# Layer 1, last block: the gate as an item of the weights' stream, second weights ahead of the half sums, the context tile third

## The chip, the cores and the metric

The kernel runs on one core of a Trainium2 chip. The time is microseconds of device time for one launch; before the change it is 1283.76 us (median of 3 runs, 1283.36 to 1283.88).

## The reference, cut to what matters

Two layers; the second one (layer 1) ends with a squared-ReLU MLP, an adaLN gate, a residual add and the final RMSNorm:

```python
def squared_relu_mlp(h, w1, w2):
    a = jax.nn.relu(h @ w1)
    return (a * a) @ w2
...
        x = x + g1 * mix
        h = rms_norm(x, norm2_g[l]) * (1 + sc2) + sh2
        x = x + g2 * squared_relu_mlp(h, w_ff1[l], w_ff2[l])
    return rms_norm(x, final_g), ckv_list, kpe_list
```

512 latent tokens and 128 context tokens, D = 1024, D_FF = 4096. Latent and context tokens have different gates g2.

## The kernel before, in words

Tokens stand in five tiles of 128: 0 to 3 are latent, 4 is context. Every product in float32 is made of three matmuls: each operand is split into a high part (rounded to fp32r) and a low part (the rest), and `mm3` (L823 to L825) adds high·high, high·low and low·high in one PSUM bank. There are six such banks for this part of the program.

A weight comes through the class `Weights`, a stream of items in a fixed order. `loads` issues the load of a raw tile on SP's queue as soon as one of five raw buffers is free (L185); `pump` takes the next item, lets ACT write the high part (L213) and lets DVE subtract it for the low part (L223). With no engine for the low part, ACT writes the negated high part (L216) and a DMA from GpSimd's queue adds the raw weight from HBM to it (L220). DVE's subtraction is put in a list, `lag`, and issued by `lows` at the next `pump`, so that ACT's copy is done by then. The first weights of layer 1's later blocks are items `w1s`: quarter combinations of one block, seven for each half block p (ACT L576, DVE L581 and, for the sources, L583).

The MLP has eight blocks of 512 hidden columns. In layer 1 the up-projection of a block's half (`up7`) is seven products of twelve matmuls of 320 columns in place of eight, with DVE adds between them (L1632); ACT makes relu, square and the high part, DVE the low part (L1637 to L1644). The down-projection (`down_t`) takes a token tile t and a half q of the 1024 output columns: four k, twelve matmuls of 512 columns. Before each block's down-projection four "half sums" (k = 0 and 1 only, six matmuls each) are made for the first four pairs (t, q), while the second half block's activations are still being made.

All engines run their instructions in the order in which this code emits them; a transfer queue keeps its order as well. In the last block (b = 7) the order is written out by hand: the gate row of the latent tokens (`gate_load(0)`, L2020) is loaded into a raw buffer before the second half block; `more` puts eight multiplications y·gate (L2032), two after each of four steps, and for each a GpSimd DMA that adds the residual x from HBM to y (L2033), between the steps of that half block. After the half sums come the context gate and the final gain (L2020, L2024), and then the pairs in the order of LASTS = (4, 3, 2, 0, 1). For tile 4 y gets the product's sum first and the gate after it (L1738, L2032); for the others the sum is multiplied by the gate and added to y (`last_more`: L2042, L2043). `last_sq` squares on ACT (L2057) and multiplies by the gain on DVE (L2059); `last_out` makes the reciprocal root and scales and stores. The first `last_out` is for three tiles together.

Of the kernel before, what the change touches and what calls it, by code (L numbers as in the profile page):

```python
# [44 lines left out]
POOL_AT = 6  # L45
H512 = slice(0, 512)
TAIL = slice(0, 256), slice(256, 512)
PARKS = 0, 1, 4, 3, 2
PARK_AT = {(0, 4): 1, (0, 5): 1, (0, 6): 1, (0, 7): 1, (1, 4): 1, (1, 5): 2, (1, 6): 2, (1, 7): 1}
MID = {6: (2, 1, 0, 3)}  # L50
# [81 lines left out]
class Weights:  # L132
# [3 lines left out]
    def __init__(self, nc, raw):  # L136
        self.nc, self.raw = nc, raw
        self.items, self.loaded, self.done = [], 0, 0
        self.raw_live, self.raw_cap, self.tiles, self.of = 0, RAWB, {}, {}
        self.raws = {}  # L140
        self.slots = None
        self.caps = {}

        self.lo = nc.vector
        self.own = {}
        self.hold = None
        self.slow = ()
        self.later, self.skip = [], False
        self.keep, self.second = {}, None
        self.lag, self.lagging = [], False  # L150
# [40 lines left out]
    def pump(self, n=1):  # L191

        if self.skip:
            self.skip = False
            return
        while n > 0 and self.done < len(self.items):
            self.lows()
            key, loads, size, use = self.items[self.done]
            own = self.own.get(key)
            if (use is None or key[0] == "w1s") and own is None and self.full(key) or key == self.hold:  # L200
                return
            self.loads()
            if self.done not in self.raws:
                return
            ts = self.raws.pop(self.done)
            if use is None:
                if own is None:
                    self.of[key], w = self.slots.take([128, 2, 1024], F32R)
                else:
                    w = own()  # L210
                r = ts[0][:, 0:size]
                hi, lo = w[:, 0, 0:size], w[:, 1, 0:size]
                self.nc.scalar.activation(out=hi, in_=r, func=AF.Copy)  # L213
                eng = None if key[0] in self.slow else self.lo
                if eng is None:
                    self.nc.scalar.activation(out=lo, in_=hi.bitcast(F32), func=AF.Copy, scale=-1.0)  # L216
                    src, shape = loads[0]
                    if len(shape) == 2:
                        lo = lo.rearrange("p (k n) -> p k n", k=shape[0])
                    self.nc.gpsimd.dma_start(out=lo, in_=src, accum_op=ALU.add)  # L220
                else:
                    self.lag.append(
                        lambda: eng.tensor_tensor(out=lo, in0=r, in1=hi.bitcast(F32), op=ALU.subtract)  # L223
                    )
                self.tiles[key] = w
                rest = None
            else:
                rest = use(ts)
            self.done += 1
            for f in self.later:  # L230
                f[0] -= 1
            self.flush(0)
            if rest:

                self.skip = False
                d = self.done
                self.pump()
                rest()
                self.skip = self.done > d
            n_raw = self.keep.pop(key, len(loads))  # L240
            self.lag.append(lambda: self.used(n_raw))
            if not self.lagging:
                self.lows()
            n -= 1
# [42 lines left out]
def body(ctx, tc, a):  # L287
# [316 lines left out]
    def add_w2(l, b):  # L604
        for k in range(FB):
            r = (b * FB + k) * 128
            st.add(("w2", l, b, k), [(a["w_ff2"][l, r:r + 128, :], (1024,))], 1024)

    add_w1(0, 0)
    vm = vmods(1)  # L610
    for b in range(1, NFB + 1):
# [13 lines left out]
    for b in range(NFB):  # L625
        if b >= 2:
            add_w1s(1, b)
        add_w2h(1, b)


# [838 lines left out]
    def mlp(l, C, H, lead, CL, per_d, per_c, mid, tick=None, turn=None, seven=False):  # L1469
# [124 lines left out]

        def up7(b, p, last=False):
            n = C[0][1]
            gates = [(t, q) for t in LASTS[1:] for q in range(2)] if last else []

            def more(k=1):
                for t, q in gates[0:k]:  # L1600
# [49 lines left out]
            p1 = new("p1")  # L1650
            act(out=p1, in_=pa, func=AF.Copy)
            pd = product(1, 2, None, True)
            st.pump()
            pb = product(2, 1, None, True)
            u2, u3 = new("u2"), new("u3")
            add(u2, p1, pb)
# [27 lines left out]
        def blocks7(f0):  # L1684

            st.lagging = True
            for b in range(NFB):
                if b >= f0:
                    for p in range(FB // 2):
                        if b == NFB - 1 and p:  # L1690
                            gate_load(0, rawp.tile([128, 1024], F32, tag="raw", name="G"))
                        up7(b, p, b == NFB - 1 and p == 1)

                cut = (lambda todo: {i: down_t(b, *i, H512, None, False, (0, 1)) for i in todo})
                if b < f0:
                    for k in (2 * b, 2 * b + 1):
                        bg.add(sums(k, room(k)))
                if b < NFB - 1:
                    todo = [(t, q) for q in range(2) for t in LASTS]
                    early = cut(todo[0:4]) if b >= f0 else {}  # L1700
                    for j, (t, q) in enumerate(todo):
                        ps = early.pop((t, q), None)
                        ps = down_t(b, t, q, H512, ps, True, range(FB) if ps is None else (3, 2))
                        y = tile_q(t, q)
                        if b == 3 and j == 0:
                            gate_rows()
                        if b == 0:
                            act(out=y, in_=cols(ps), func=AF.Copy)
                        else:
                            vec.tensor_tensor(out=y, in0=cols(ps), in1=y, op=ALU.add)  # L1710
                        bg.step(2)
                        if j == 4:
                            free2(b, 0)
                        if j:
                            st.pump(1 + j % 2)
                    free2(b, 1)
                    if b == f0 - 1:
                        bg.drain()
                    continue

                todo = [(t, q) for t in LASTS for q in range(2)]
                st.pump(4)
                early = cut(todo[0:4])
                w = st.slots.take([128, 2, 1024], F32)[1]
                gate_load(1, w[:, 0])
                gain_load(w[:, 1])
                zs = [fa.tile([128, 2, T], F32, tag="aa", name="z").rearrange("p a n -> p (a n)") for _ in range(3)]
                st.slots.free += cell["spare"]
                zs += [st.slots.take([128, 2, 1024], F32)[1].rearrange("p a n -> p (a n)") for _ in range(2)]
                cell["zs"] = [z[:, 0:1024] for z in zs]  # L1730
                for t, q in todo:
                    i = LASTS.index(t)
                    for v in TAIL if (t, q) == todo[-1] else (H512,):
                        ps = early.pop((t, q), None)
                        ps = down_t(b, t, q, v, ps, True, range(FB) if ps is None else (3, 2))
                        if not i:
                            y = tile_q(t, q)
                            vec.tensor_tensor(out=y, in0=cols(ps), in1=y, op=ALU.add)  # L1738
                            last_gate(t, (q,))
                        else:  # L1740
                            last_more(t, q, v, ps)
                            last_sq(t, q, v, q + (v.start > 0))
                    if q and i == 2:

                        for k in range(2):
                            last_sq(LASTS[0], k, H512, k)
                        last_out(LASTS[0:3], False)
                    elif q and i > 2:
                        last_out(LASTS[i:i + 1], i == 4)

        spare = []

# [266 lines left out]
    def gate_load(m, out):  # L2019
        nc.sync.dma_start(out=out, in_=grow[m:m + 1, :].to_broadcast([128, D]))  # L2020
        cell["G", m] = out
# [23 lines left out]
    def last_sq(t, q, v, i):  # L2045
# [1 line left out]
        k = slice(v.start // 128, v.stop // 128)  # L2047
        y = tile_q(t, q)[:, k]
        if (t, "ss") not in cell:
            i3 = LASTS.index(t)  # L2050
            if ("ss", i3 // 3) not in cell:
                cell["ss", i3 // 3] = sc.tile([128, 8], F32, tag="m", name=f"ss{t}", bufs=10)
            cell[t, "ss"] = cell["ss", i3 // 3][:, i3 % 3 * 2:]
            cell[t, "z"] = cell["zs"].pop(0)
# [4 lines left out]
        vec.tensor_tensor(out=cols(cell[t, "z"][:, u]), in0=y, in1=cols(cell["fg"][:, u]), op=ALU.mult)  # L2059

    def last_out(ts, both):
        i3, n = LASTS.index(ts[0]), len(ts)
        ss = cell["ss", i3 // 3]
        i3 %= 3
        sm = sc.tile([128, 8], F32, tag="m", name=f"sm{ts[0]}", bufs=10)[:, 0:n]
# [14 lines left out]
                eng.dma_start(out=a["y"][tok(t), u], in_=y)  # L2080

    xT = dr.tile([T, D], F32, name="xT")
    grow = dr.tile([2, D], F32, name="grow")
    LASTS = (4, 3, 2, 0, 1)

    def pool_mm(ci, N, gs=POOL_ORDER):
# [184 lines left out]
```

## Time and profile before

| | |
|---|---|
| median of 3 runs | 1283.76 us |
| the profiled execution itself | 1285.38 us |
| its span, first to last instruction | 1283.6 us |
| TensorE (PE) busy | 1247.0 us, 97% |
| VectorE (DVE) busy | 796.9 us, 62% |
| ScalarE (ACT) busy | 571.1 us, 44% |
| GpSimd (POOL) busy | 198.5 us, 15% |
| TensorE's mean granted clock | 0.988 of full speed |

The span is what the profile's views count from; 1.8 us of the profiled execution lie outside it, and the execution is 1.6 us above the median. PE's share is an average: the stretch to look at is the last block, from about 1219 us to the end. There a row of a timeline reads: start, duration, engine, line of the kernel, operation, tiles out<-in, shape, and in brackets the idle time before it and what ended that. A matmul's duration overlaps that of the next one, so the distance between two starts is what one costs.

### The profile page before, as it was taken

The numbers are of one execution on the slowest core, as the hardware profiler recorded it, in microseconds if no ns is written. First come the engines' busy times: TensorE is split into PE (matmuls) and PEld (weight loads), VectorE is DVE, ScalarE is ACT, GpSimd is POOL, SyncE is SP. The second block draws the span as 40 slices with busy tenths as digits, with TensorE's granted clock in tenths as the row PEclk, the third lists the DMA queues.
The fourth block names the chain that finished last, engine by engine and source line by source line (L and its number), as shares of the span: only waits on it lengthen the run. The fifth ranks groups of instructions, "written<-read, shape, count | busy, mean of one in ns | idle before, by whom it ended". The sixth has DMA issues, their size and how long they took to land. (4 is left out here: it accounts for less than half of the span.)

```text
span 1283.6 us, 19571 instructions
## 1 busy us (share of the span) xinstructions
PE 1247.0 (97%) x7744; PEld 1135.7 (88%) x7744; DVE 796.9 (62%) x1455; ACT 571.1 (44%) x1022; POOL 198.5 (15%) x181
## 2 busy tenths in 40 slices
PE   6999999999999999999999999899999999999986
PEld 4899975689999999999999999889898989989875
DVE  5753854554766566666666637775576556675667
ACT  4445654543554434334332424745444515445154
POOL 0010122212122221313131314210000000000030
PEclk9999999999999999999999999899999999999988
DMA  7752696250344443535353441904113343132273
GB/s 297 262 167 68 152 254 235 97 197 1 120 139 139 124 154 119 158 121 159 120 161 118 142 139 29 234 27 128 60 33 100 83 82 96 37 122 76 66 128 102
DMA packets 79163, 161.89 MB, mean 126 GB/s; under 512 B 7728, under 2 KB 34864, under 8 KB 78560
## 3 DMA queue, kind: packets, MB, share of 16 engines
q1 hardware_dynamic: 69296, 145.94, 35.6%
q0 software_dynamic: 9344, 14.35, 6.2%
q8 instruction: 61, 1.00, 0.3%
q10 hardware_dynamic: 432, 0.35, 0.1%
q14 instruction: 30, 0.25, 0.1%
HBM read 149.46 MB, written 8.02 MB: 123 GB/s over the span
## 5 line engine op out<-in xcount | busy, mean ns | idle before, releaser
L823 PE MATMUL up_ps<-h,w 128*128 128x320 f32 (+2 forms) x800 | 251.8, 315 | 4.7 <-DVE r L1632 3.1
L824 PE MATMUL up_ps<-h,w 128*128 128x320 f32 (+2 forms) x800 | 249.4, 312 | 1.2 <-DVE h L774 1.2
L825 PE MATMUL up_ps<-h,w 128*128 128x320 f32 (+2 forms) x800 | 249.9, 312 | 0.0
L213 ACT ACTIVATE w<-raw 128x1024 fp32r<-128x1024 f32 (+4 forms) x131 | 132.8, 1027 | 109.6 <-DMA raw<-w_ff 84.1
L223 DVE TENSOR_TENSOR w<-raw,w 128x1024 fp32r<-128x1024 f32 (+4 forms) x122 | 151.5, 1249 | 48.0 <-ACT w L213 47.1
L823 PEld LDWEIGHTS up_ps<-h,w 128*128 128x128 f32 x800 | 152.4, 190 | 9.1 <-issue 6.7
L823 PE MATMUL dn_ps<-aa,w 128*128 128x328 f32 (+1 forms) x512 | 159.1, 311 | 0.0
L824 PE MATMUL dn_ps<-aa,w 128*128 128x328 f32 (+1 forms) x512 | 159.0, 311 | 0.0
L825 PE MATMUL dn_ps<-aa,w 128*128 128x328 f32 (+1 forms) x512 | 158.1, 309 | 0.0
L824 PEld LDWEIGHTS up_ps<-h,w 128*128 128x128 f32 x800 | 152.7, 191 | 1.9 <-DVE h L774 1.6
L825 PEld LDWEIGHTS up_ps<-h,w 128*128 128x128 f32 x800 | 152.2, 190 | 0.3 <-DMA w<-w_ff 0.3
L484 POOL TENSOR_TENSOR acc<-acc,raw 128x1024 f32<-128x1024 f32 x42 | 100.7, 2397 | 303.7 <-ACT raw L482 303.7
L824 PE MATMUL dn_ps<-w,aa 128*128 128x512 f32 (+1 forms) x324 | 126.1, 389 | 2.4 <-DVE w L223 2.4
L823 PE MATMUL dn_ps<-w,aa 128*128 128x512 f32 (+1 forms) x324 | 126.8, 391 | 0.0
L825 PE MATMUL dn_ps<-w,aa 128*128 128x512 f32 (+1 forms) x324 | 126.3, 390 | 0.0
L1429 DVE SCALAR_TENSOR_TENSOR x<-dn_ps,mod,x 128x328 f32<-128x328 f32 (+2 forms) x168 | 67.3, 435 | 68.0 <-PE dn_ps L825 67.3
L576 ACT ACTIVATE w<-raw 128x512 fp32r<-128x512 f32 x84 | 51.0, 625 | 120.5 <-DVE raw L583 120.5
L823 PEld LDWEIGHTS dn_ps<-aa,w 128*128 128x128 f32 x512 | 96.4, 188 | 1.8 <-ACT r L1502 0.8
L825 PEld LDWEIGHTS dn_ps<-aa,w 128*128 128x128 f32 x512 | 96.3, 188 | 0.0
L824 PEld LDWEIGHTS dn_ps<-aa,w 128*128 128x128 f32 x512 | 96.2, 188 | 0.1
L482 ACT ACTIVATE raw<-raw,cs 128x1024 f32<-128x1024 f32 x42 | 48.3, 1150 | 62.5 <-DVE acc L477 58.0
L824 PEld LDWEIGHTS dn_ps<-w,aa 128*128 128x128 f32 x324 | 61.3, 189 | 15.5 <-DVE w L223 2.8
(403 smaller groups left out, 2421.1 us busy)
## 6 DMA issues: line engine op xcount, KB each, us to landing
raw<-w_ff SPq DMA_DIRECT2D x126, 512.0 KB, 3.8
raw<-w_mod SPq DMA_DIRECT2D x80, 512.0 KB, 3.9
raw<-w_m SPq DMA_DIRECT2D x16, 512.0 KB, 6.5
raw<-w_out SPq DMA_DIRECT2D x8, 512.0 KB, 4.5
w<-w_ff POOLq DMA_DIRECT2D x8, 512.0 KB, 9.8
kT<-ckvT POOLq DMA_DIRECT2D x4, 768.0 KB, 11.0
xr<-x SPq DMA_DIRECT2D x5, 512.0 KB, 6.2
xs<-x SPq DMA_DIRECT2D x2, 1280.0 KB, 10.1
```

The source lines that it names most:

```text
L213: self.nc.scalar.activation(out=hi, in_=r, func=AF.Copy)
L223: lambda: eng.tensor_tensor(out=lo, in0=r, in1=hi.bitcast(F32), op=ALU.subtract)
L482: act(out=raw if k else acc[1], in_=raw, func=AF.Copy, scale=w[1])
L484: nc.gpsimd.tensor_tensor(out=acc[1], in0=acc[1], in1=raw, op=ALU.add)
L576: act(out=w[:, 0], in_=src, func=AF.Copy)
L823: mm(ps, lhsT=st_[0], rhs=mv[0], start=first, stop=False, skip_group_check=on)
L824: mm(ps, lhsT=st_[0], rhs=mv[1], start=False, stop=False, skip_group_check=on)
L825: mm(ps, lhsT=st_[1], rhs=mv[0], start=False, stop=last, skip_group_check=on)
L1429: vec.scalar_tensor_tensor(out=xv, in0=ps[:, p0:p0 + c1 - c0], scalar=gate[:, d, m:m + 1], in1=xv, op0=ALU.mult, op1=ALU.add)
```

## The change

The latent tokens' gate is an item `("gate",)` of the stream, ahead of the last block's second weights; it has no work of its own, and its raw buffer is kept to the end (`keep` 0). The first two second weights of that block (k = 0 and 1, both halves q) get their low part by ACT and a GpSimd DMA (`st.dma`) in place of DVE. One pump in the last half block takes two items, so all four second weights are pumped before the half sums, and `lows` issues the last subtraction there too. The order is ENDS = (3, 2, 4, 0, 1); the gate multiplications of tiles 3, 2 and 0 stay in the half block, those of tiles 4 and 1 come behind the half sums; tile 4 goes the way of the others (`last_more`, `last_sq`).

```diff
+ENDS = 3, 2, 4, 0, 1
...
-                eng = None if key[0] in self.slow else self.lo
+                eng = None if key[0] in self.slow or key in self.dma else self.lo
...
+        if b == NFB - 1:
+
+            st.add(("gate",), [(grow[0:1, :].to_broadcast([128, D]), (D,))], 0, lambda ts: cell.update({("G", 0): ts[0]}))
+            st.keep["gate",] = 0
+            st.dma = [("w2", 1, b, 0, h) for h in range(2)]
         add_w2h(1, b)
...
-            gates = [(t, q) for t in LASTS[1:] for q in range(2)] if last else []
+            gates = [(t, q) for t in ENDS[0:2] + ENDS[3:4] for q in range(2)] if last else []
...
             pd = product(1, 2, None, True)
-            st.pump()
+            st.pump(1 + last)
             pb = product(2, 1, None, True)
...
-                        if b == NFB - 1 and p:
-                            gate_load(0, rawp.tile([128, 1024], F32, tag="raw", name="G"))
...
-                todo = [(t, q) for t in LASTS for q in range(2)]
-                st.pump(4)
+                todo = [(t, q) for t in ENDS for q in range(2)]
+                st.pump(5)
+                st.lows()
                 early = cut(todo[0:4])
...
+                last_gate(NT - 1)
+                last_gate(ENDS[-1])
                 for t, q in todo:
-                    i = LASTS.index(t)
+                    i = ENDS.index(t)
...
-                        if not i:
-                            y = tile_q(t, q)
-                            vec.tensor_tensor(out=y, in0=cols(ps), in1=y, op=ALU.add)
-                            last_gate(t, (q,))
-                        else:
-                            last_more(t, q, v, ps)
-                            last_sq(t, q, v, q + (v.start > 0))
-                    if q and i == 2:
-
-                        for k in range(2):
-                            last_sq(LASTS[0], k, H512, k)
-                        last_out(LASTS[0:3], False)
-                    elif q and i > 2:
-                        last_out(LASTS[i:i + 1], i == 4)
+                        last_more(t, q, v, ps)
+                        last_sq(t, q, v, q + (v.start > 0))
+                    if q and i >= 2:
+                        last_out(ENDS[0:3] if i == 2 else ENDS[i:i + 1], i == 4)
```

The lines of the changed kernel are numbered a little otherwise (L581 is L582, L1632 is L1639, L2032 is L2030, L823 to L825 are L830 to L832, L220 is L221, L2033 is L2031). On DVE, in the last half block, from the low part of the sixth w1s item on (w<-raw,w 128x512: a w1s low part; x: y; u, r: adds of the up-projection; 128x1024: a second weight's low part). Before:

```order
L581 TENSOR_TENSOR w<-raw,w 128x512
L1632 TENSOR_TENSOR u_11701<-p_11671,up_ps 128x320
L1632 TENSOR_TENSOR u_11702<-u_11701,up_ps 128x320
L2032 TENSOR_TENSOR x_2778<-x_2778,G 128x4x128
L2032 TENSOR_TENSOR x_2779<-x_2779,G 128x4x128
L581 TENSOR_TENSOR w<-raw,w 128x512
L1632 TENSOR_TENSOR r<-u_11702,up_ps 128x320
```

And of the change:

```order
L582 TENSOR_TENSOR w<-raw,w 128x512 x2
L1639 TENSOR_TENSOR u_11704<-p_11669,up_ps 128x320
L1639 TENSOR_TENSOR u_11705<-u_11704,up_ps 128x320
L2030 TENSOR_TENSOR x_2779<-x_2779,raw 128x4x128
L2030 TENSOR_TENSOR x_2780<-x_2780,raw 128x4x128
L1639 TENSOR_TENSOR r<-u_11705,up_ps 128x320
```

The seventh w1s item's low part moves ahead of the two adds u; the gate is now a tile of the raw pool. On GpSimd's queue, from the first transfer of the last block on (x<-xT adds the residual to half a tile of y, in the order t, q). Before:

```order
L2033 DMA x_2778<-xT 128x4x128
L2033 DMA x_2779<-xT 128x4x128
L2033 DMA x_2778<-xT 128x4x128
L2033 DMA x_2779<-xT 128x4x128
L2033 DMA x_2778<-xT 128x4x128
L2033 DMA x_2779<-xT 128x4x128
```

And of the change:

```order
L2031 DMA x_2779<-xT 128x4x128
L2031 DMA x_2780<-xT 128x4x128
L221 DMA w<-w_ff 128x2x512
L2031 DMA x_2779<-xT 128x4x128
L2031 DMA x_2780<-xT 128x4x128
L221 DMA w<-w_ff 128x2x512
L2031 DMA x_2779<-xT 128x4x128
```

The low parts of the first two second weights stand third and sixth in a queue that held residuals alone. On PE, the first half sum and the start of the second, with what each waits for (DVE, Activation, DMASW5 and DMASW0 are semaphores; the DMASW ones count GpSimd's transfers, and these two are those of the two w<-w_ff above). Before:

```order
L825 MATMUL up_ps<-h_8166,w 128x320
L823 MATMUL dn_ps<-w,aa 128x512 [waits Activation_49]
L824 MATMUL dn_ps<-w,aa 128x512 [waits DVE_49]
L825 MATMUL dn_ps<-w,aa 128x512
L823 MATMUL dn_ps<-w,aa 128x512
L824 MATMUL dn_ps<-w,aa 128x512
L825 MATMUL dn_ps<-w,aa 128x512
L823 MATMUL dn_ps<-w,aa 128x512 [waits Activation_49]
L824 MATMUL dn_ps<-w,aa 128x512 [waits DVE_49]
```

And of the change:

```order
L832 MATMUL up_ps<-h_8166,w 128x320
L830 MATMUL dn_ps<-w,aa 128x512 [waits Activation_49]
L831 MATMUL dn_ps<-w,aa 128x512 [waits DMASW5_49,Activation_49]
L832 MATMUL dn_ps<-w,aa 128x512
L830 MATMUL dn_ps<-w,aa 128x512
L831 MATMUL dn_ps<-w,aa 128x512
L832 MATMUL dn_ps<-w,aa 128x512
L830 MATMUL dn_ps<-w,aa 128x512 [waits Activation_49]
L831 MATMUL dn_ps<-w,aa 128x512 [waits DMASW0_49,Activation_49]
```

The second matmul of each of the first two half sums waited for DVE; now it waits for one of those transfers.

## Rows read from the trace of the kernel before

**Rows 1.** Timeline of PE in the last block (columns as told above).

```profile
1230.67 0.31 PE L825 MATMUL up_ps<-room,w 128*128 128x320 f32 x1
1234.09 0.60 PE L823 MATMUL up_ps<-h,w 128*128 128x320 f32 x1 [3.11 <-DVE r L1632]
...
1240.47 0.40 PE L823 MATMUL dn_ps<-w,aa 128*128 128x512 f32 x1
...
1247.29 0.39 PE L823 MATMUL dn_ps<-w,aa 128*128 128x512 f32 x1
1250.10 0.50 PE L824 MATMUL dn_ps<-w,aa 128*128 128x512 f32 x1 [2.42 <-DVE w L223]
...
1251.21 0.63 PE L824 MATMUL dn_ps<-w,aa 128*128 128x512 f32 x1
1251.64 0.63 PE L825 MATMUL dn_ps<-w,aa 128*128 128x512 f32 x1
...
1254.31 0.40 PE L823 MATMUL dn_ps<-w,aa 128*128 128x512 f32 x1
...
1255.24 0.39 PE L824 MATMUL dn_ps<-w,aa 128*128 128x512 f32 x1
```

**Rows 2.** Timeline of DVE in the last block.

```profile
1227.23 0.68 DVE L581 TENSOR_TENSOR w<-raw,w 128x512 fp32r<-128x512 f32 x1
1227.83 0.48 DVE L1632 TENSOR_TENSOR u<-p,up_ps 128x320 f32<-128x320 f32 x1
1228.35 0.49 DVE L1632 TENSOR_TENSOR u<-u,up_ps 128x320 f32<-128x320 f32 x1
1231.64 1.29 DVE L2032 TENSOR_TENSOR x<-x,G 128x512 f32<-128x512 f32 x2 [2.81 <-DMA G<-grow]
...
1248.83 1.22 DVE L223 TENSOR_TENSOR w<-raw,w 128x1024 fp32r<-128x1024 f32 x1
...
1254.51 0.69 DVE L2042 TENSOR_TENSOR gy<-dn_ps,G 128x512 f32<-128x512 f32 x1 [0.79 <-PE dn_ps L825]
...
1256.57 0.68 DVE L2042 TENSOR_TENSOR gy<-dn_ps,G 128x512 f32<-128x512 f32 x1
...
1266.24 0.68 DVE L2042 TENSOR_TENSOR gy<-dn_ps,G 128x512 f32<-128x512 f32 x1
```

**Rows 3.** Timeline of ACT, from the last half block's seventh w1s item.

```profile
1227.01 0.62 ACT L576 ACTIVATE w<-raw 128x512 fp32r<-128x512 f32 x1
1227.54 1.99 ACT L213 ACTIVATE w<-raw 128x1024 fp32r<-128x1024 f32 x2
```

**Rows 4.** Timeline of SP's queue, 1227 to 1235 us.

```profile
1227.98 0.34 SPq L2020 DMA_DIRECT2D G<-grow  x1
```

**Rows 5.** Timeline of GpSimd, 1232 to 1260 us.

```profile
1232.96 10.47 POOL L2033 DMA_DIRECT2D x<-xT  x8 [380.77 <-DVE x L2032]
```

**Rows 6.** Transfers issued at 1232.96, 1254.32, 797.54 us: queue, KB, us to landing.

```profile
x<-xT POOLq DMA_DIRECT2D x1, 256.0 KB, 9.7
...
x<-xT POOLq DMA_DIRECT2D x1, 256.0 KB, 4.6
...
w<-w_ff POOLq DMA_DIRECT2D x1, 512.0 KB, 6.2
```

**Rows 7.** Packets, 1238 to 1240 us (q1: SP's queue, q0: GpSimd's).

```profile
q1 hardware_dynamic: 96, 0.38, 77.7%
q0 software_dynamic: 103, 0.05, 22.6%
```

**Rows 8.** Windows: length, engines' busy us (instructions), granted clock, DMA share, GB/s.

```profile
1234.00:1240.00 6.00, 5.91 (x22) 5.95 (x23) 6.00 (x10) 4.85 (x9) 6.00 (x6) 0.50 0.87 203
...
1250.50:1253.50 3.00, 3.00 (x9) 2.35 (x8) 1.16 (x2) 0.00 (x0) 0.00 (x0) 0.50 1.42 177
...
1244.00:1250.00 6.00, 3.68 (x17) 2.71 (x15) 2.47 (x3) 0.00 (x0) 0.79 (x1) 1.00 1.45 181
...
831.00:832.00 1.00, 1.00 (x9) 1.00 (x8) 0.46 (x2) 0.61 (x2) 0.00 (x0) 1.00 1.10 203
```

More of the change, by code (lines that the diff above doesn't have):

```diff
@@ L146, in __init__ @@
         self.hold = None
-        self.slow = ()
+        self.slow, self.dma = (), ()
         self.later, self.skip = [], False
@@ L607, in add_w2 @@
             st.add(("w2", l, b, k), [(a["w_ff2"][l, r:r + 128, :], (1024,))], 1024)
+    grow = dr.tile([2, D], F32, name="grow")
     add_w1(0, 0)
@@ L2049, in last_sq @@
         if (t, "ss") not in cell:
-            i3 = LASTS.index(t)
+            i3 = ENDS.index(t)
             if ("ss", i3 // 3) not in cell:
@@ L2061, in last_out @@
     def last_out(ts, both):
-        i3, n = LASTS.index(ts[0]), len(ts)
+        i3, n = ENDS.index(ts[0]), len(ts)
         ss = cell["ss", i3 // 3]
@@ L2082, in body @@
     xT = dr.tile([T, D], F32, name="xT")
-    grow = dr.tile([2, D], F32, name="grow")
     LASTS = (4, 3, 2, 0, 1)
```

## The prediction

> **What bounds the kernel now.** I read the last block in the timelines, first PE's, then those of the engines that PE waits for. PE is the bound until shortly before the end: it does nothing but matmuls, except for two waits. The first: a matmul of the last half block starts at 1230.67, the next at 1234.09, released by DVE's add r (L1632), 3.1 us late by the bracket [rows 1]. DVE was late because its gate multiplication stood still for 2.81 us, until the gate had landed, with that add behind it in its order [rows 2]; the gate's load was issued at 1227.98, once a raw buffer was free [rows 4]. The second: the half sums run from 1240.47, and at 1247.29 PE stops until 1250.10 for a second weight's low part (L223) [rows 1], which DVE starts at 1248.83 [rows 2], behind the add and the gate of tile 4. Each wait leaves PE slow: granted clock 0.50 (the 1.2 GHz level) from 1234 to 1240 and from 1250.5 to 1253.5, 1.00 from 1244 to 1250 [rows 8]. A 512-column matmul costs 0.43 us at the low level (1251.21 to 1251.64) and 0.23 at the full one (four from 1254.31 to 1255.24) [rows 1]. From the first complete sum on, DVE's multiplication at 1254.51 [rows 2], DVE has three operations for each half tile, and it soon is the bound itself up to the last store.
>
> So there are some 11 us to be had: 3.3 and 2.6 of waiting, about 3 for 24 matmuls at half speed (6.4 us from 1234.09 to 1240.47, half of it too much) and 2.0 for ten at 0.43.
>
> **The change part by part.**
>
> *Gate in the stream.* Its load takes the place of the first second weight's in SP's queue, which was issued during the block before; it lands long before 1229, and DVE's 2.81 us go. The second weights move down one place: the first two still come early (before, ACT took the first two without a pause at 1227.54 [rows 3]), the last two when the last w1s item gives its raw buffers back at about 1229; ACT wants them at about 1233. Nothing waits there.
>
> *A pump of two items.* The last w1s low part moves ahead of the two adds u. ACT's high part for it ends at 1227.63 [rows 3], so DVE runs it at 1227.83, where the first u stood; one such step costs 0.60 (1227.23 to 1227.83 [rows 2]), so the u's, and with them PE's fifth product, come 0.6 later. The gates of tile 3 follow from 1229.4 (second u at 1228.95) in place of 1231.64, and r behind them ends at 1231.1. The fifth product ends at 1230.67 + 0.6 + 0.15 = 1231.4, so the sixth does not wait for r any more. Two products of twelve at 0.15 bring the half sums to 1234.9, 5.5 us before 1240.47. The price on ACT, two more copies of 1.0 us (1.99 for two [rows 3]), delays only the activations of k = 3 and 2, which the half sums don't use.
>
> *Low parts by transfer.* This is the part that decides. DVE is rid of two subtractions of 1.22 [rows 2], and the second matmul of the first half sum, and that of the second one, now wait for a transfer of GpSimd's queue. That queue holds, in this order: two residuals of tile 3, weight, two residuals of tile 2, weight. I go through it:
> - First issue: before, 1.32 us after the first gate multiplication started (1231.64 to 1232.96 [rows 2, 5]); now 1229.4 + 1.3 = 1230.7. An issue takes 1.31 (eight in 10.47 [rows 5]), so the weights are issued at 1233.3 and 1237.1.
> - First residual: alone it lands 4.6 us after its issue, before the change it took 9.7 [rows 6]. Of the 4.6, 1.45 is moving (256 KB at 181 GB/s [rows 8]), some 2.4 before and 0.75 behind. The 9.7 came from the context gate and the final gain, 1 MB on SP's queue. While they run the 16 engines move one packet for GpSimd (0.05 MB in 103, 512 bytes each) for one of SP's (0.38 MB in 96, 4 KB each) [rows 7]. Those two loads come now too, behind the last second weight, when PE's fifth product frees their slot at 1231.4: 256 packets at 48 per us, from about 1232.6 to 1237.9. The residual moves from 1233.1: some 247 of its 528 packets until 1237.9, the rest in 0.8 us, landed at 1239.4 (8.7 us, nearer to 9.7 than to 4.6, since the same loads are beside it).
> - From there the queue moves without a pause: second residual 1.45, weight 2.6 (512 KB at 203 GB/s [rows 8], the fastest us of such transfers), so the first weight is there at 1243.4; two residuals 2.9 and a weight 2.6: the second is there at 1248.9.
>
> *PE behind it.* It stops at 1235.1, does six matmuls at 1243.5, stops again, and has 17 of the 24 of the half sums left at 1249.0. At the full clock these take 3.9 us. After the two waits of before the clock was low for about 3.9 us (back by 1254.31 [rows 1]) and for 6 us [rows 8]; 17 matmuls then take 5.7 or 6.7. I take 6.2: half sums done at 1255.2, first complete sum 6 matmuls (1.4) and 0.1 later, and DVE's first multiplication at 1256.7 in place of 1254.51: 2.2 late.
>
> *All second weights ahead.* The last low part is done on DVE at about 1241, under PE's wait, and so are the gates of tiles 4 and 1 (four of 0.61). The second wait of before is gone; the new one costs more.
>
> *Tile third.* Before 1254.51 DVE had tile 4 done but for two gain multiplications; now all of it comes behind. Before, the four halves to the next root and the first multiplication of the tile after it took 11.7 us (1254.51 to 1266.24), of which 4 x 2.06 (1254.51 to 1256.57) for the halves [rows 2]; the other 3.5 are the root, 1.2 for two gain multiplications and about 0.6 of waiting for PE. Now six halves, 12.4, and the root, 1.7: 14.1, so 2.4 more. PE keeps ahead: its sixth half is there 11.0 us after the half sums (four of 1.4, two of 2.7), DVE gets to it after 11.8. Behind that, both kernels do the same.
>
> The sum: 2.2 + 2.4 = 4.6 us more than the profiled execution's own 1285.38. By the median, 1283.76, it is 1288.4.
>
> The ends: if the loads on SP's queue did not slow GpSimd's at all (4.6 for the first residual), the second weight would be there at 1244.9, the multiplication at 1252.1, 2.4 early, and the sum nothing: 1283.8. With 9.7 for the first residual, 3.05 for each weight (6.2 alone [rows 6] less the 3.15 that aren't moving) and 6.7 for the 17 matmuls, the multiplication comes at 1259.1, 4.6 late: 7.0 in all, 1290.8.
>
> **The rivals.**
>
> *The transfers overlap.* Faster: if a weight's transfer did not stand in line behind the residuals but landed 6.2 us after its own issue, as one with nothing ahead of it did [rows 6], the second would be there at 1243.3. With PE's waits that short, and the full clock for the 17 matmuls, the multiplication comes at 1248.8, 5.7 early: 3.3 less in all, 1280.5. It decides where the second weight lands before about 1245. For it: the issues are done by 1238. Against it: before, transfers issued 1.3 apart landed in their order while the queue moved 181 GB/s, and the first itself took 9.7.
>
> The Trainium skill (DMA: Bandwidth & Descriptors, Anatomy of one DMA, SWDGE path) gives 2.0 us plus the bytes at 436 GB/s for one transfer of GpSimd's, 3.2 us for a weight. By it the second would be there at 1240.3, the multiplication at 1245.8, and the time would be 1277.5. The trace does not agree for these transfers: they add to what they find, and 181 and 203 GB/s are what they moved.
>
> *SP's loads don't interfere*, because they pass before the first residual's packets: the lower end above, 1283.8. For it: only if their slot is free earlier than I think; against it, the two queues start within a us of each other.
>
> *The clock stays up.* The 17 matmuls then take 3.9, 2.3 less than I take: 1286.1. Against it: both waits of before, far shorter than the 8 us here, had it fall.
>
> That the gate still comes late I leave out; its load is issued a whole half block before it is read.
>
> **How the numbers follow.** Forecast 0.66, 1288.4, its own range 1286.4 to 1290.8; overlap 0.13; no interference 0.13; clock up 0.08. A measurement of this kernel can tell about 0.2%, 2.6 us, from no change: the forecast is slower, the last two are the same, overlap is faster. Slower 0.66, same 0.21, faster 0.13. The range is 1283.0 to 1290.8: it takes in all but the overlap and a little above.
>
> **What would show it.** In the profile after: no wait of DVE for the gate, PE without a stop until 1235; then two waits of PE at its half sums (L831) released by a GpSimd transfer, of about 8 and 4 us, with the clock at 0.50 behind them; x<-xT taking 8 to 10 us for the first; DVE's first multiplication by the gate from a sum (L2040) at 1256 or so, no wait of PE for a second weight's subtraction (L224), and DVE without gaps from there on. I am wrong if the second weight lands before 1245, or if PE goes from the last product into the half sums with less than 3 us of waiting.

## The result and the profile after

The changed kernel takes 1291.91 us, median of four runs (1290.50 to 1293.11), beside 1283.82 (four runs, 1283.36 to 1285.01) for the kernel before: ratio 1.0061, 95% interval 1.0044 to 1.0079, so 5.6 to 10.1 us slower. The forecast was 1288.4, its range ended at 1290.8. The side was right; the size, 4.6 us for 8.1, was not. The profiled execution took 1291.59 us, its span is 1289.8.

PE in the last block of the changed kernel, the answer to [rows 1] (start, duration, engine, line, operation, tiles, shape, idle time before and its releaser):

```profile
1231.52 0.39 PE L830 MATMUL up_ps<-w 128*128 128x320 f32 x1 [0.78 <-DVE u L1639]
...
1236.87 0.39 PE L830 MATMUL dn_ps<-w,aa 128*128 128x512 f32 x1
...
1245.62 0.77 PE L831 MATMUL dn_ps<-w,aa 128*128 128x512 f32 x1 [8.36 <-DMA w<-w_ff]
...
1247.89 0.63 PE L830 MATMUL dn_ps<-w,aa 128*128 128x512 f32 x1
1251.09 0.77 PE L831 MATMUL dn_ps<-w,aa 128*128 128x512 f32 x1 [2.58 <-DMA w<-w_ff]
...
1257.42 0.39 PE L830 MATMUL dn_ps<-w,aa 128*128 128x512 f32 x1
```

The first row starts the fifth product, the last one follows the half sums. The two old waits are gone, for the gate and for DVE's subtraction; two new ones stand at the half sums, both released by a transfer of a second weight, 8.4 and 2.6 us. DVE in the same stretch, the answer to [rows 2]:

```profile
1231.29 1.29 DVE L2030 TENSOR_TENSOR x<-x,raw 128x512 f32<-128x512 f32 x2
...
1241.42 1.22 DVE L224 TENSOR_TENSOR w<-raw,w 128x1024 fp32r<-128x1024 f32 x1
...
1258.98 0.69 DVE L2040 TENSOR_TENSOR gy<-dn_ps,raw 128x512 f32<-128x512 f32 x1 [13.94 <-PE dn_ps L832]
...
1272.84 0.68 DVE L2040 TENSOR_TENSOR gy<-dn_ps,raw 128x512 f32<-128x512 f32 x1
```

The gate's multiplication (first row) waits for nothing; the first complete sum comes at 1258.98, tile 0's first multiplication at 1272.84. The transfers, each with its KB and its time from issue to landing (issued 1232.58 and 1234.13; before, [rows 6]), and the windows with the granted clock, the third number from the end (before, [rows 8]):

```profile
x<-xT POOLq DMA_DIRECT2D x1, 256.0 KB, 8.9
...
w<-w_ff POOLq DMA_DIRECT2D x1, 512.0 KB, 11.4
```

```profile
1238.00:1244.00 6.00, 0.00 (x0) 0.00 (x0) 3.60 (x7) 2.85 (x7) 5.39 (x5) 0.88 1.22 240
1244.00:1250.00 6.00, 2.90 (x6) 1.82 (x6) 1.04 (x2) 0.00 (x0) 4.75 (x4) 0.50 1.29 193
1250.00:1256.00 6.00, 4.91 (x12) 3.88 (x13) 0.00 (x0) 0.00 (x0) 0.00 (x0) 0.50 1.44 180
```

While PE stands, the granted clock falls to 0.50, the 1.2 GHz level, and stays there to 1256: a matmul of the half sums costs 0.43 there.

All of this stands where the forecast put it, but for the second wait, which is 2.6 us in place of 4. What does not fit is at the top: the fifth product starts at 1231.52 where 1229.6 was expected: 0.6 for the larger pump, behind the start that PE's timeline of the kernel before has, in a row that is not among [rows 1]:

```profile
1228.98 0.38 PE L823 MATMUL up_ps<-w 128*128 128x320 f32 x1 [0.19 <-DVE u L1632]
```

The whole last block begins 1.9 us late, though both programs are in the same order up to there. That set the question for the runs: does the change cost something upstream, or was the kernel before not measured where I thought?

### The profile page after: what moved, and what is told of

Same layout as the page of the kernel before. It is cut to its first block, busy times and chain, and to the rows that moved or that the text cites. A ratio compares the mean times of both kernels' runs of the same rounds, so it can differ in the third digit from the quotient of the medians.

```text
span 1289.8 us, 19581 instructions
## 1 busy us (share of the span) xinstructions
PE 1248.1 (97%) x7744; PEld 1134.9 (88%) x7744; DVE 795.5 (62%) x1455; ACT 573.1 (44%) x1024; POOL 201.1 (16%) x183
## 5 line engine op out<-in xcount | busy, mean ns | idle before, releaser
L830 PE MATMUL up_ps<-h,w 128*128 128x320 f32 (+2 forms) x800 | 250.1, 313 | 2.2 <-ACT h L777 1.5
L832 PE MATMUL up_ps<-h,w 128*128 128x320 f32 (+2 forms) x800 | 248.5, 311 | 0.0
L830 PE MATMUL dn_ps<-aa,w 128*128 128x328 f32 (+1 forms) x512 | 159.1, 311 | 0.0
L832 PE MATMUL dn_ps<-aa,w 128*128 128x328 f32 (+1 forms) x512 | 158.1, 309 | 0.0
L830 PEld LDWEIGHTS up_ps<-h,w 128*128 128x128 f32 x800 | 151.0, 189 | 6.8 <-issue 3.4
L832 PEld LDWEIGHTS up_ps<-h,w 128*128 128x128 f32 x800 | 150.8, 189 | 0.2 <-DMA w<-w_ff 0.2
L830 PE MATMUL dn_ps<-w,aa 128*128 128x512 f32 (+1 forms) x324 | 127.4, 393 | 0.0
L832 PE MATMUL dn_ps<-w,aa 128*128 128x512 f32 (+1 forms) x324 | 127.1, 392 | 0.0
L830 PEld LDWEIGHTS dn_ps<-aa,w 128*128 128x128 f32 x512 | 96.4, 188 | 1.8 <-ACT r L1509 0.8
L832 PEld LDWEIGHTS dn_ps<-aa,w 128*128 128x128 f32 x512 | 96.3, 188 | 0.0
L483 ACT ACTIVATE raw<-raw,cs 128x1024 f32<-128x1024 f32 x42 | 48.3, 1150 | 63.4 <-DVE acc L478 58.9
```

The lines of the kernel that those rows point to most:

```text
L483: act(out=raw if k else acc[1], in_=raw, func=AF.Copy, scale=w[1])
L830: mm(ps, lhsT=st_[0], rhs=mv[0], start=first, stop=False, skip_group_check=on)
L832: mm(ps, lhsT=st_[1], rhs=mv[0], start=False, stop=last, skip_group_check=on)
```

## The experiments

Two spans are compared in all profiles: from the first matmul of the fifth product (first row above) to DVE's first multiplication of a complete sum by the gate, and to the end of the span. All times are in us; a ratio is to the kernel before, measured beside it. A complete sum is a finished down-projection of half a tile; in the old order of tiles the context tile is done ahead of the first such multiplication, in the new one behind it, so kernels of different order are compared by the way to the end.

| kernel | fifth product to first multiplication | to the end | median | ratio (95%) |
|---|---|---|---|---|
| before, five profiles | 25.5, 20.8, 21.1, 24.0, 22.2 | 54.6, 49.9, 50.1, 53.0, 51.2 | 1283.8 to 1286.4 | 1 |
| changed, two profiles | 27.5, 27.5 | 58.3, 58.4 | 1291.9, 1291.5 | 1.0061, 1.0059 (1.0042 to 1.0076) |
| low parts on DVE, twice | 14.2, 14.2 | 45.3, 45.3 | 1278.8, 1279.6 | 0.9956 (0.9940 to 0.9972), 0.9948 (0.9936 to 0.9959) |
| the same, old order of tiles | 15.1 | 44.0 | 1279.0 | 0.9945 (0.9931 to 0.9959) |
| gate only | 19.0 | 48.4 | 1280.8 | 0.9976 (0.9965 to 0.9987) |
| weights ahead of residuals | 20.8 | 51.6 | 1284.8 | 1.0002 (0.9989 to 1.0014) |
| no row loads | 24.5 | 55.4 | 1288.4 | 1.0031 (1.0018 to 1.0044) |
| two gates' tiles on GpSimd | 14.7 | 48.3 | 1281.3 | 0.9976 (0.9962 to 0.9991) |

Of the five in the first row the first is the profile shown ahead of the prediction; the third belongs to the kernel with the DRAM tile allocated first, whose instructions and order are the same.

### Is the change late upstream?

One line moved in the kernel before, the part of the change that acts from the start of the program:

```diff
+    grow = dr.tile([2, D], F32, name="grow")
     add_w1(0, 0)
...
     xT = dr.tile([T, D], F32, name="xT")
-    grow = dr.tile([2, D], F32, name="grow")
```

> The kernel before with one line moved: the small DRAM tile of the gate rows is allocated ahead of the blocks, as the change needs it. It executes the same instructions in the same order. Theory that the 2 us upstream come from run to run: the same time as the kernel before within 0.1%, 1283.5 to 1285.5 us. Rival (the tile's place in DRAM, or another address behind it, slows something early): 1286 to 1288 us, with the last block 2 us late.

Measured: 1284.38, ratio 0.9998 (0.9986 to 1.0009). The tile's place costs nothing that can be seen. The gate's item, which is in the stream from the block before on, is the other part that could act ahead of the fifth product. It is in the nine profiles of the kernels with it: they start the fifth product at 1229.9 to 1234.5, mean 1231.8, which is 1.0 behind the mean of the five without it, and 0.6 of that is the larger pump. What is left, 0.4, is well inside the scatter. Beside the moved line the kernel before again:

> The kernel before, unchanged, profiled a second time. If the 2 us by which the changed kernel's profile is late already at the start of the last block are run to run, two profiles of this one program differ by as much there: the last half block's fifth product may start anywhere from 1229 to 1231 us. If they come from the change, this profile has it at 1229.0 within 0.5 us.

Measured: 1284.12, ratio 1.0006 (0.9994 to 1.0019). Its profile, and then that of the DRAM tile's run:

```profile
1230.94 0.39 PE L823 MATMUL up_ps<-w 128*128 128x320 f32 x1 [0.20 <-DVE u L1632]
1235.68 0.39 PE L823 MATMUL up_ps<-h,w 128*128 128x320 f32 x1 [2.74 <-DVE r L1632]
1248.91 0.50 PE L824 MATMUL dn_ps<-w,aa 128*128 128x512 f32 x1 [2.42 <-DVE w L223]
1251.78 0.69 DVE L2042 TENSOR_TENSOR gy<-dn_ps,G 128x512 f32<-128x512 f32 x1
```

```profile
1233.70 0.39 PE L824 MATMUL up_ps<-w 128*128 128x320 f32 x1 [0.19 <-DVE u L1633]
1238.67 0.39 PE L824 MATMUL up_ps<-h,w 128*128 128x320 f32 x1 [2.97 <-DVE r L1633]
1251.90 0.50 PE L825 MATMUL dn_ps<-w,aa 128*128 128x512 f32 x1 [2.42 <-DVE w L223]
1254.77 0.69 DVE L2043 TENSOR_TENSOR gy<-dn_ps,G 128x512 f32<-128x512 f32 x1
```

Two things are to be seen. The fifth product starts at 1230.94 and 1233.70 in a program where [rows 1] belong to a start at 1228.98: so much is run to run. And the same two waits as there (2.74 or 2.97, and 2.42) are not followed by slow matmuls: the first row behind the first wait lasts 0.39, not 0.60. (The three columns at the end of a window are the granted clock, the DMA share and GB/s.) Windows from the end of each wait on, first in the profile ahead of the prediction, then in the second profile of the same program:

```profile
1234.10:1240.40 6.30, 6.30 (x24) 6.30 (x25) 6.30 (x11) 5.12 (x10) 6.30 (x6) 0.51 0.89 212
1250.10:1254.30 4.20, 4.20 (x11) 3.35 (x12) 1.38 (x2) 0.00 (x0) 0.39 (x1) 0.59 1.19 149
```

```profile
1235.70:1239.10 3.40, 3.40 (x23) 3.40 (x24) 3.40 (x6) 3.00 (x6) 3.40 (x4) 1.00 0.85 198
1248.90:1251.90 3.00, 2.99 (x13) 2.45 (x14) 1.47 (x3) 0.00 (x0) 0.40 (x1) 1.00 1.45 181
```

About as many matmuls (24 and 23) take 6.3 us at a granted clock of 0.51, or 3.4 us at 1.00. The second stretch is 1.5 us shorter as well, from the wait's end to the first multiplication (4.41 and 2.87). Two more profiles of the kernel before:

> The kernel before, one more profile. Three profiles of its program so far had the same two waits of PE in the last block (2.7 to 3.1 and 2.4 us); in one, the first, TensorE's granted clock fell to 0.50 behind them and the way from the fifth product to the first multiplication took 25.5 us, in two it stayed 1.00 and that way took 20.8 and 21.1 us. If the fall is a matter of the single execution, it may show either here; if it belongs to the first profile alone, 21 us.

> The same as the look before it: either 21 us with the clock at 1.00 behind the waits, or 23 to 26 us with a fall to 0.50 behind one or both.

Measured: 24.0 and 22.2 us. First the one, then the other, in the same windows behind the two waits (2.79 and 2.42, 2.81 and 2.42), and behind them two rows of the one, the end of its first wait and its first slow matmul:

```profile
1233.50:1238.50 5.00, 5.00 (x24) 5.00 (x25) 5.00 (x8) 4.57 (x8) 5.00 (x6) 0.66 0.97 209
1248.20:1252.60 4.40, 4.38 (x12) 3.46 (x13) 1.39 (x2) 0.00 (x0) 0.57 (x2) 0.61 1.45 181
```

```profile
1236.50:1241.50 5.00, 5.00 (x25) 5.00 (x26) 5.00 (x8) 4.56 (x8) 5.00 (x6) 0.72 0.91 205
1251.00:1253.80 2.80, 2.80 (x12) 2.34 (x13) 1.31 (x2) 0.00 (x0) 0.38 (x1) 1.00 1.45 181
```

```profile
1233.45 0.39 PE L823 MATMUL up_ps<-h,w 128*128 128x320 f32 x1 [2.79 <-DVE r L1632]
...
1235.01 0.47 PE L824 MATMUL up_ps<-h,w 128*128 128x320 f32 x1
```

So behind the same waits of 2.4 to 3.1 us the clock falls in one execution and not in the next: behind the first wait in three of five, behind the second in two. The profile on which the prediction rests has both falls, the first one whole, and the longest way of the five to the first multiplication, 25.5 against a mean of 22.7. Its total is near the median all the same, because it began that block early: the five start the fifth product at 1228.7 to 1233.7, mean 1230.8. Its long way, 2.8 us above the mean and most of it the clock's, and its early start, 1.8 us ahead of the mean, stood against each other in one execution. The two earliest starts of the five go with the two longest ways; whether that is chance five executions do not tell.

The control of the changed kernel:

> The changed kernel, unchanged, as a control beside the two. By my theory its last block costs 4 to 5 us and the rest is run to run: 1288 to 1290 us, 4 to 5 over the kernel before in the same runs. Rival (the first measurement was right): 1292 us, 8 over it. In the profile the last block itself should repeat: PE's two waits at its half sums of about 8 and 2.6 us, the first multiplication of DVE from a complete sum 27.5 us after the fifth product's first matmul, each within 0.5 us.

Measured: 1291.50, and 27.5 us again: PE's waits are 8.11 and 2.72. The time is the rival's, and the repeat of the block is as I expected. Behind waits of 4.8 to 8.4 us the fall came in each of the four profiles that have them, the two of the changed kernel and two of those below (weights ahead, 5.17; no row loads, 4.79).

### What the two transfers cost

```diff
             st.keep["gate",] = 0
-            st.dma = [("w2", 1, b, 0, h) for h in range(2)]
```

> The changed kernel, but the low parts of the first two second weights are subtracted on DVE again, not by a transfer of GpSimd's. My theory: those two transfers are the whole cost, and the other parts of the change gain. PE does not stop between its products and the half sums nor in them (no wait over 1 us at L831); the first complete sum's gate multiplication comes about 11 us earlier than in the kernel before, the stretch of tiles after it is 2.4 us longer: about 1275 us, 0.7% under the kernel before. If all of the last block starts 2 us late here too, as in the changed kernel, 1277. Rival (the order with tile 4 third and all second weights ahead is what costs): not under 1284 us, and DVE is late with the half sums' weights in place of the transfers.

Measured: 1278.80, 13 us under the changed kernel and 5.6 under the kernel before. PE goes from the products into the half sums without a wait and runs at full clock, and DVE has the first complete sum 13.3 us sooner after the fifth product than in the changed kernel:

```profile
1237.00:1245.00 8.00, 8.00 (x37) 6.65 (x36) 7.15 (x12) 4.08 (x8) 4.20 (x4) 1.00 1.31 219
```

```profile
1245.90 0.68 DVE L2039 TENSOR_TENSOR gy<-dn_ps,raw 128x512 f32<-128x512 f32 x1
...
1259.74 0.68 DVE L2039 TENSOR_TENSOR gy<-dn_ps,raw 128x512 f32<-128x512 f32 x1
```

The transfers are the whole loss; the rival falls. The time is 4 us above the 1275 expected, and 2 above the 1277 for a late start, which it has here too (the fifth product starts at 1231.74). The base found above accounts for it: counted from the mean of the five, 45.3 + 0.6 against 51.8, the gain should be 5.9.

### Does the queue stand in line, and for what?

```diff
             add(u3, u2, pd)
-            more(2)
             st.pump()
...
             add(out(g, 1), u3, pc)
-            more(2)
             st.pump()
+            more(2)
```

`more` makes the gate multiplications on DVE too, so these come later with the residuals.

> The changed kernel with the two second weights' transfers issued ahead of all residuals in GpSimd's queue. If the queue moves its transfers one after the other (my theory), the first lands some 9 to 10 us and the second some 11 to 12 us after the first issue, PE stops once for about 5 us and goes on: about 1282 us, 10 under the changed kernel's 1292. Rival (such a weight's transfer takes 11 to 15 us by itself, wherever it stands): landings 11 to 15 us after their issues, 1287 us or more.

Measured: 1284.77, some 7 us under the changed kernel where I expected 10, and 3 over the 1282 expected. The landings of the two weights, and PE's two waits for them:

```profile
w<-w_ff POOLq DMA_DIRECT2D x1, 512.0 KB, 5.9
...
w<-w_ff POOLq DMA_DIRECT2D x1, 512.0 KB, 10.6
```

```profile
1237.43 0.47 PE L831 MATMUL dn_ps<-w,aa 128*128 128x512 f32 x1 [0.64 <-DMA w<-w_ff]
...
1244.24 0.76 PE L831 MATMUL dn_ps<-w,aa 128*128 128x512 f32 x1 [5.17 <-DMA w<-w_ff]
```

A weight with nothing ahead of it in GpSimd's queue lands 5.9 us after its issue, not 11 to 15, so the rival falls: the rest came from where it stood, behind two residuals and by then beside the row loads. The second one took longer than I gave it. From 1237.5 to 1240, between the two weights, SP's queue moved 159 packets and GpSimd's one; why GpSimd's stood still was not tested. The Trainium skill (DMA: Bandwidth & Descriptors, Anatomy of one DMA, SWDGE path) would have each weight land in 3.2 us by its 2.0 us plus bytes at 436 GB/s, an estimate, and a residual of 256 KB in 2.6. The 5.9 had loads on SP's queue beside it, but the residual of 4.6 in [rows 6] had none, so the figure does not hold for these adding transfers.

```diff
-                gate_load(1, w[:, 0])
-                gain_load(w[:, 1])
+                cell["G", 1] = cell["fg"] = cell["G", 0]
```

> The changed kernel without the two loads of the context gate and the final gain (1 MB on SP's queue); the latent gate's row stands in for both, so that part of the result is left out. If these loads share the DMA engines packet for packet with GpSimd's queue (my theory), the first residual lands 4.6 to 5 us after its issue in place of 8.9, and both weights about 4 us earlier: 1287 to 1288 us. Rival (GpSimd's queue is slow by itself): landings as in the changed kernel (8.9, 11.4 and 14.6 us after issue), 1292 us.

Measured: 1288.40, ratio 1.0031. The first residual and the first weight:

```profile
x<-xT POOLq DMA_DIRECT2D x1, 256.0 KB, 4.2
...
w<-w_ff POOLq DMA_DIRECT2D x1, 512.0 KB, 7.8
```

4.2 in place of 8.9, 7.8 in place of 11.4, and 1288.40 in place of 1292: 1 MB on SP's queue holds GpSimd's queue up by some 4 us, and the rival falls. The size is the one that the prediction's count of packets gives, but the packets did not go as counted. In the changed kernel one for one holds only from 1235 to 1237 (75 of SP's, 75 of GpSimd's); the two us after that (q1 is SP's queue, q0 GpSimd's):

```profile
q1 hardware_dynamic: 37, 0.12, 55.6%
q0 software_dynamic: 76, 0.04, 33.3%
...
q0 software_dynamic: 182, 0.09, 75.4%
q1 hardware_dynamic: 48, 0.16, 44.7%
```

So a share per packet is not a rule to carry away: with the weights ahead it was 159 to 1, here it went down to 48 to 182.

### The other parts of the change

```diff
+    grow = dr.tile([2, D], F32, name="grow")
...
+        if b == NFB - 1:
+            st.add(("gate",), [(grow[0:1, :].to_broadcast([128, D]), (D,))], 0, lambda ts: cell.update({("G", 0): ts[0]}))
+            st.keep["gate",] = 0
...
-            st.pump()
+            st.pump(1 + last)
...
-                        if b == NFB - 1 and p:
-                            gate_load(0, rawp.tile([128, 1024], F32, tag="raw", name="G"))
...
-    grow = dr.tile([2, D], F32, name="grow")
```

> The kernel before with one part of the change: the latent gate is an item of the weights' stream (with the pump of two items, so that the weights keep their places), nothing else. My theory: DVE's 2.8 us of waiting for the gate and PE's 3.1 us behind it go, with most of the slow clock behind them; the second wait of PE (about 2.5 us, for the last second weight's low part) stays: about 1278 us. Rival (DVE's wait only moves to something else in the block, or the last stretch is DVE's bound whenever it begins): 1283 to 1285 us.

Measured: 1280.83, 3.1 us under the kernel before, where some 6 were expected (1278). PE's first wait is gone and the second, 2.42 us, is there; the clock was 0.50 from 1247 to 1250 behind it. 48.4 + 0.6 against the mean of 51.8 is 2.8: the same error in the base accounts for it.

The old order of tiles, in the kernel with the gate only:

```diff
-                st.pump(4)
+                st.pump(5)
+                st.lows()
```

> The kernel before with the gate as a stream item and all four second weights handled ahead of the half sums, low parts on DVE, but the tiles in the old order (the context tokens' tile first, its sum added ahead of its gate). It takes the tile order out of the best version so far (1278.8 us). Theory: that order is worth little once no wait is left, since DVE has the same work in the stretch: from the fifth product to the first multiplication of tile 0 28.0 us with the new order, 27.3 here (the multiplication of the first tile's gate hides under PE); 1278 us, within 1 us of the version with the new order. Rival (the order costs what DVE's stretch grew by, 2 us): 1276.5 us.

> The changed kernel with all low parts on DVE, once more, beside the version with the old order of tiles, on the same chip: 1278.8 us again, within 1.5.

Measured: 1278.99 and 1279.58; to tile 0's first multiplication 26.8 and 28.0 us. The order of the tiles is worth 1.2 us in the profiles, and its 0.6 in the medians can't be told from nothing. The 1.2 lies between the theory's 0.7 and the rival's 2 and does not decide between them; either way the order matters little with the low parts on DVE.

### A failed improvement

In the version without transfers, DVE takes four gate multiplications just ahead of the first complete sum. I gave them to GpSimd (`last_gate` takes the engine):

```diff
-                last_gate(NT - 1)
-                last_gate(ENDS[-1])
+                last_gate(NT - 1, eng=nc.gpsimd)
+                last_gate(ENDS[-1], eng=nc.gpsimd)
```

> The changed kernel with the first two second weights' low parts on DVE, and the last two tiles' gate multiplications (four of 0.61 us, just ahead of the first complete sum) moved from DVE to GpSimd, which is idle there. In the version without this move DVE reached the first complete sum at 1245.9, 2 us after PE had it, and was the bound to the end. Theory: DVE begins 2 us earlier and stays the bound, 1276 to 1277 us. Rival (GpSimd's multiplications, 1.5 us or more each, and its issues behind them bring the residuals of the third tile late, or slow DVE): 1279 us or more.

Measured: 1281.30, 2.5 us over the version without it: the rival's time. Three of GpSimd's four multiplications; DVE's work beside them; and the three subtractions of its first row as the second profile of the kernel before has them:

```profile
1241.34 3.51 POOL L2029 TENSOR_TENSOR x<-x,w 128x512 f32<-128x512 f32 x1
...
1248.86 1.79 POOL L2029 TENSOR_TENSOR x<-x,raw 128x512 f32<-128x512 f32 x1
...
1251.76 1.82 POOL L2029 TENSOR_TENSOR x<-x,raw 128x512 f32<-128x512 f32 x1
```

```profile
1243.64 4.47 DVE L1650 TENSOR_TENSOR aa<-r,aa 128x320 fp32r<-128x320 f32 x3
...
1249.17 0.68 DVE L2039 TENSOR_TENSOR gy<-dn_ps,raw 128x512 f32<-128x512 f32 x1
...
1251.24 2.89 DVE L2056 TENSOR_TENSOR z<-x,w 128x512 f32<-128x512 f32 x1
```

```profile
1243.67 1.28 DVE L1644 TENSOR_TENSOR aa<-r,aa 128x320 fp32r<-128x320 f32 x3
```

Three subtractions that took 1.28 in the second profile of the kernel before take 4.47, and a multiplication of 0.69 takes 2.89. The one that reads its first operand from PSUM (gy, beside GpSimd's of 1248.86) keeps its 0.68. The Trainium skill (SBUF — State Buffer, SBUF: two separate sides) has GpSimd and DVE lock a shared pair of ports against each other for a whole instruction where DVE reads two operands from SBUF; the rows agree in which of DVE's instructions are slow, and no run here shows the lock itself.

## Why the prediction was wrong

By its own steps, with 1.94 us added for the later start of the fifth product:

- *Gate in the stream, pump of two.* Right: no wait for the gate; half sums expected at 1236.84, seen at 1236.87.
- *Low parts by transfer.* Right in each size: first residual 8.7 us, seen 8.9 (by luck in part: SP's loads ran on past 1240, where the count has them through at 1239.8, and GpSimd's packets went faster beside them than one for one); first weight there at 1245.3, PE goes on at 1245.62; second at 1250.8, PE goes on at 1251.09; the 17 matmuls behind it 6.2 us, seen 6.3 (1251.09 to 1257.42). First multiplication at 1258.6, seen at 1258.98. The second wait came out at 2.6, not 4, because the six matmuls between ran at the low clock, for which the prediction had the full one (1.4 us for the six).
- *Tile third.* 14.1 us to tile 0's first multiplication, seen 13.86. From the first multiplication to the end of the span the changed kernel takes 30.8, before 29.1: 1.7 us, not 2.4.
- *The sum.* Here it failed. The term that failed is the first, the 2.2: it sets the new first multiplication against that of one execution of the kernel before, 1254.51, as if that were the program's. The prediction counts "some 11 us to be had" there, of which "about 3 for 24 matmuls at half speed" and "2.0 for ten at 0.43" lie behind the two waits. Those 5 us do not belong to every execution: two of the five profiles had neither fall, one had only the second with part of the first, one part of the first alone. The forecast's own first multiplication, 27.7 us behind the old start of the fifth product, is 2.2 late against the one execution that had both, but 27.7 - 22.7 = 5.0 late against the mean of five. With 2.4 behind it that makes 7.4 and 1291.2 on the median given, where 1291.9 was measured. The runs have 27.5 + 0.6 - 22.7 = 5.4 for this term and 1.7 for the tail, 7.1 in all.

In short, a term of the sum was mis-sized: what the kernel before loses to the clock, which was read from one execution. The new waits of 8 us bring the fall in every profile of the changed kernel, so it pays each time for what the old one pays by chance. The same correction, applied to the other kernels (to the end plus 0.6, less 51.8), gives 7.1 for the changed one, -5.9 for low parts on DVE, -7.2 for the old order with them, -2.8 for the gate only, +0.4, +4.2 and -2.9 for the last three; each lies in the interval of its ratio. With the 54.6 of the first profile in place of 51.8 every one of these is 2.8 lower, and none lies in its interval. The mean rests on five executions that spread over 4.7 us, so it is good to a us or so.

What stays open is why the clock falls behind a wait in one execution and not in another. The length of the wait does not tell: 2.97 had no fall, 2.79 had one. The tail came out at 1.7, though tile 0 comes 2.1 later after the first multiplication (13.86 for 11.73); the 0.4 between them lies behind the issue of the last store, from which the kernel before takes 3.86 and 3.84 us to the end in two profiles, the changed one 3.47 and 3.51. Why is not shown.

## What to carry to other kernels

A profile is one execution: before a saving is taken from a slow clock behind a short wait, look whether a second profile of the same program has it, and put the sum on the mean of the stretch that changes and not on the single one. The longer waits here, 4.8 us and more, brought the fall each time and could be priced. A transfer put on a queue behind others costs what stands ahead of it and beside it on the other queue; here two subtractions of 1.2 us were taken off DVE and 11 us of PE's waiting came in their place.

The best version here leaves the low parts on DVE: 1278.8 to 1279.6 us, 5.6 to 7.1 us under the kernel before by the ratios, with either order of the tiles.

## What was not expected of the hardware

- The granted clock in the same program: behind equal waits 0.51 or 1.00. It differs far upstream too. From 24 to 28 us, the profile ahead of the prediction and then the second profile of the same program:

```profile
24.00:28.00 4.00, 4.00 (x31) 2.97 (x30) 3.25 (x7) 1.92 (x3) 0.00 (x0) 1.00 1.01 405
```

```profile
24.00:28.00 4.00, 4.00 (x12) 3.30 (x11) 3.18 (x5) 1.91 (x3) 0.00 (x0) 0.50 0.84 340
```

The 15 matmuls of 480 columns that begin at 23.83 in the one and 23.40 in the other take 3.4 and 6.0 us to the start of what follows. That is one way in which two executions of one program can come to the last block 2 us apart; that it is what made these 2 us is not shown.

- GpSimd's multiplication beside DVE's work: 3.51 us for the first, 1.82 for the last, and DVE's three subtractions 4.47 in place of 1.28.
